# Two of the four sums of weight quarters made by accumulating DMAs in place of VectorE adds

## The chip, the cores and the metric

One core of a Trainium2 chip runs the whole program in one launch. The metric is the device time in microseconds; before the change the median of three runs is 2033.21 us (2032.05 to 2033.67). One execution was profiled.

## What is computed

Two decoder layers on 512 tokens of width 1024. Each has a feed-forward, a mixer and a second feed-forward; the mixer is gated linear attention in the first layer and latent attention in the second, with a cross-attention to 256 memory tokens beside it.

```python
for i in range(DEPTH):
    x = x + 0.5 * swiglu(rmsnorm(x, ffn1_norm[i]), ffn1_w_gate[i], ffn1_w_up[i], ffn1_w_down[i])
    h = rmsnorm(x, mix_norm[i])
    ...
    x = x + jnp.concatenate([o, o_mem], axis=-1) @ w_out[i]
    x = x + 0.5 * swiglu(rmsnorm(x, ffn2_norm[i]), ffn2_w_gate[i], ffn2_w_up[i], ffn2_w_down[i])

def swiglu(h, w_gate, w_up, w_down):
    return (jax.nn.silu(h @ w_gate) * (h @ w_up)) @ w_down
```

The change touches the weights of `w_gate` and `w_up` alone. Each of the four feed-forwards has 22 column blocks of 128 in each of them, taken two at a time: 44 groups in the program.

## The kernel before

All arithmetic is float32, made from pairs. A tile is split into a rounded high part (`fp32r`) and the rest, and a product is three matmuls: high by high, high by rest, rest by high (`mm3`). For a weight tile the high part `wh` is a cast on ScalarE and the rest `wl` a subtraction on VectorE; both read a raw tile of 128 by 1024 that a DMA from SP's queue brought from `wflat`, 512 KB.

The gate and up products of a group are made by a scheme with seven products in place of eight. The two weight blocks are cut into halves of the contracted width, which gives four quarters: a11 (gate, upper half), a21 (up, upper), a22 (up, lower), a12 (gate, lower). Seven left operands are made of them: a11, s1 = a21 + a22, s2 = s1 + a11, a12, s3 = a21 + a11, s4 = s2 + a12, and a22. VectorE makes the four sums, s3 in place on a21's raw tile, s1 and s2/s4 in two `sum` tiles. Each operand is split into `wh` and `wl` and used by 24 matmuls of 256 columns (`seven`, which also forms the sums of the activations in the same manner on VectorE and ScalarE: the tiles `t`). One group is thus 168 matmuls. Between groups stand steps of the down projection of the chunk of blocks before (`down`, with 512 columns and one plain weight unit per eight tiles), as `CHUNKS` and `SHARES` (lines 38 and 39) tell: none between the first two groups of a feed-forward, and one to three units between later ones.

The buffers are: four raw tiles, two sum tiles, four pairs of `wh` and `wl` (line 37). A raw tile's next load waits until its last reader is done; a pair is free once TensorE has made the product that reads it.

The order of each engine's queue is written by a planner in the kernel (`Flows`, lines 163 to 285): generators yield operations, the planner keeps a clock for each engine, prices every operation (`price`, line 140) and takes the one that can start first. The framework then moves instructions about by its own estimate when it writes the program. The queues are in order on the chip: an instruction that waits holds all that stands behind it on its engine. Since every operation is issued in `make` (line 136), all rows of the profile have that line, and are told apart by their tiles.

`load_unit` (line 348) issues one raw load per quarter or plain unit, and `split_weights` (line 357) makes sums and splits. `start` (line 1542) issues the first loads between the eight tiles of x.

Of the kernel before, what the change touches and what calls it, by code (L numbers as in the profile page):

```python
# [9 lines left out]
F32 = mybir.dt.float32  # L10
# [4 lines left out]
ALU = mybir.AluOpType  # L15
AX = mybir.AxisListType

P = 128
# [15 lines left out]
XH, XDH = 4, 128  # L34
UMAX = 1024
BLOCK = 256
NRAW, NSUM, NSPL, NTMP = 4, 2, 4, 31
CHUNKS = (4, 6, 4, 8)
SHARES = ((0, 0), (2, 2, 4), (4, 4), (2, 2, 2, 2))
HS = S // 2  # L40
# [60 lines left out]
def _n_free(a):  # L101
    return int(np.prod(a.shape[1:]))


def _in_psum(a):
    return a.space == bass.MemoryType.PSUM
# [13 lines left out]
class Engine:  # L120
# [19 lines left out]
    def price(self, method, kw, outs, ins):  # L140
        n = max([_n_free(outs[0])] + ([_n_free(ins[0])] if method == "tensor_reduce" else []))
        if self.name == "PE":
            if method == "transpose":
                return 110, 200
            n = _n_free(kw["rhs"])
            return (n / 2.4 + 13.3 if ins[0].dtype == F32R else 4 * n / 2.4 + 10), 200
        if self.name == "ACT":
            return 100 + 0.833 * n, 130
        if self.name == "POOL":
            return 100 + 2.2 * n, 200  # L150
        if method == "dma_start":
            return 60, 2000 + 4 * P * n / 360
        if method == "tensor_tensor_scan":
            return 70 + 2.1 * n, 130
        if method == "reciprocal":
            return 65 + 6 * n, 130
        single = method in ("tensor_scalar", "tensor_copy", "tensor_scalar_mul")
        if single and not any(_in_psum(a) for a in ins[:1] + outs[:1]):
            return 70 + 0.53 * n, 110
        return 70 + 1.042 * n, 110  # L160


class Flows:
# [7 lines left out]
    def spawn(self, gen, rank=1):  # L171
        self.count += 1
        self.flows.append([rank, self.count, gen, None, True])
# [4 lines left out]
    def done(self, *tiles):  # L178
        for t in tiles:
            if t.name in self.halves:  # L180
                h = self.halves[t.name]
                i = t.offset % UMAX // (UMAX // 2)
                assert h[2][i] is None
                h[2][i] = self.used(t.name, i * UMAX // 2, (i + 1) * UMAX // 2)
                if None not in h[2]:
                    del self.halves[t.name]
                    self.free_at["d"].append(max(h[2]))
            else:
                self.free_at[self.kind.pop(t.name)].append(self.used(t.name, 0, UMAX))
# [98 lines left out]
def _emit(tc, ctx, xT, memT, wflat, sizes, cst, out):  # L288
# [17 lines left out]
    V, A, G, T, Q = (Engine(e, n) for e, n in ((nc.vector, "DVE"), (nc.scalar, "ACT"), (nc.gpsimd, "POOL"),  # L306
                                               (nc.tensor, "PE"), (nc.sync, "SP")))
    spawn, done = fl.spawn, fl.done
# [3 lines left out]
    parts = [cs, None, None]  # L312

    def C(name, a=None, b=None):
        part, lo, hi = _C[name]
        if a is not None:
            lo, hi = lo + a, lo + b
        return parts[part][:, lo:hi]
# [21 lines left out]

    units = [[None, Flag()] for _ in sizes]
    outs = [[Flag(), None, n] for n, four in sizes for _ in range(7 if four == 1 else 1 if four == 0 else 0)]

    ahead = [0, 0]

    def load_unit():
        u, n = units[ahead[0]], sizes[ahead[0]][0]
        raw = yield Take("raw", F32, 0)  # L350
        o = ahead[1]
        yield Q.dma_start(out=raw[:, :n], in_=wflat[o : o + n * P].rearrange("(p n) -> p n", p=P))
        ahead[0] += 1
        ahead[1] += n * P
        u[0], u[1].set = raw, True

    def split_weights():
        def parts():
            h = yield Take("wh", F32R, 0)
            l = yield Take("wl", F32R, 0)  # L360
            return h, l

        def high(hl, src, n=UMAX):
            yield A.copy(out=hl[0][:, :n], in_=src[:, :n])

        def low(hl, src, n=UMAX):
            yield V.tensor_tensor(out=hl[1][:, :n], in0=src[:, :n], in1=hl[0][:, :n].bitcast(F32), op=ALU.subtract)
            o = outs[made[0]]
            made[0] += 1
            o[1], o[0].set = hl, True  # L370

        def add(out, a, b):
            yield V.tensor_tensor(out=out, in0=a, in1=b, op=ALU.add)

        todo = iter(zip(units, sizes))
        for u, (n, four) in todo:
            if four == 0:
                yield u[1]
                hl = yield from parts()
                yield from high(hl, u[0], n)  # L380
                yield from low(hl, u[0], n)
                done(u[0])
                continue
            u21, u22, u12 = (next(todo)[0] for _ in range(3))
            yield u[1]
            a11 = u[0]
            p = yield from parts()
            yield from high(p, a11)
            yield u21[1]
            yield u22[1]  # L390
            a21, a22 = u21[0], u22[0]
            s1 = yield Take("sum", F32, 0)
            yield from add(s1, a21, a22)
            yield from low(p, a11)
            p = yield from parts()
            yield from high(p, s1)
            s2 = yield Take("sum", F32, 0)
            yield from add(s2, s1, a11)
            yield from low(p, s1)
            done(s1)  # L400
            p = yield from parts()
            yield from high(p, s2)
            yield from add(a21, a21, a11)
            done(a11)
            yield from low(p, s2)
            yield u12[1]
            a12 = u12[0]
            p = yield from parts()
            yield from high(p, a12)
            yield from add(s2, s2, a12)  # L410
            yield from low(p, a12)
            done(a12)
            p = yield from parts()
            yield from high(p, a21)
            p2 = yield from parts()
            yield from high(p2, s2)
            yield from low(p, a21)
            done(a21)
            p = yield from parts()
            yield from high(p, a22)  # L420
            yield from low(p2, s2)
            done(s2)
            yield from low(p, a22)
            done(a22)

# [4 lines left out]
    class Blocks:  # L430
# [5 lines left out]
        def next(self):  # L436
            j = self.i % self.per
            if j == 0:
                self.end()
                u = outs[at[0]]  # L440
                assert u[2] == min(self.per, self.n - self.i) * self.w, at
                at[0] += 1
                yield u[0]
                self.cur = u[1]
            self.i += 1
            return tuple(t[:, j * self.w : (j + 1) * self.w] for t in self.cur)
# [67 lines left out]
    class Norm:  # L514
# [18 lines left out]
        def add(self, k):  # L533
            spawn(self.square(k), 1)
            yield from self.split(k)
# [134 lines left out]


    def seven(nrm, hid, f, start):

        made_, read = ({n: Flag() for n in ("p1", "p5", "u2", "p2", "u3", "p3", "p4")} for _ in range(2))
# [867 lines left out]
    def start():  # L1542
        yield V.memset(ones, 1.0)
        yield A.activation(out=warm, in_=ones[:, :1], func=AF.Silu)
        yield Q.dma_start(out=cs, in_=cst[:, : _PARTS[0]])
        spawn(split_weights(), lambda: 3 if made[0] - at[0] >= NAHEAD else -1)
        nrm = Norm("f1", 0)
        for k in range(KD):
            spawn(nrm.split(k), 0)
        for k in range(KD):  # L1550
            spawn(late_square(nrm, k))
        spawn(trunk(nrm), 2)
        yield from load_unit()
        for k in range(KD):
            yield Q.dma_start(out=x[k], in_=xT[:, k, :])
            xin[k].set = True
            if k in (3, 5, 7):
                yield from load_unit()
        yield V.tensor_scalar_mul(out=xqs, in0=C("xq"), scalar1=XDH ** -0.5)
        while ahead[0] < len(sizes):  # L1560
            yield from load_unit()

    def late_square(nrm, k):
        yield nrm.part[KD - 1]
        yield outs[NLATE][0]
        yield from nrm.square(k)

    def trunk(nrm):
        for l in range(2):
            nx = Norm("mx", l)  # L1570
            spawn(load_part(l + 1, nrm))
            yield from ffn(nrm, nx, False)
            nrm = Norm("f2", l)
            yield from (gla if l == 0 else mla)(l, nx, nrm)
            nx = Norm("f1", 1) if l == 0 else None
            yield from ffn(nrm, nx, l == 1)
            nrm = nx
# [160 lines left out]
```

## Time and profile before

| what | us |
|---|---|
| median of three runs | 2033.21 |
| the profiled execution's own time | 2034.4 |
| its span | 2032.6 |
| PE busy in the span | 2001.6 |
| DVE (VectorE) busy | 1595.5 |
| ACT (ScalarE) busy | 983.2 |
| POOL (GpSimd) busy | 49.1 |

PE is the row of the matmuls, PEld that of their weight loads, DVE is VectorE, ACT ScalarE, POOL GpSimd, SP the engine whose queue issues most DMAs. Busy shares are averages over stages with unlike limits, so the stages are looked at one by one. In a row of groups stand: line, engine, operation, tile written and tiles read, the shape, the count, then busy us and the mean ns of one, then the idle time of that engine just before them and what ended it. `sum<-raw` is s1, `raw<-raw` is s3, and `sum<-sum,raw` is s2 or s4.

### The profile page before, as it was taken

Reading aid. Unit: us, or ns where it says so; the run is one execution under the profiler, and the core shown is the slowest. Engines: PE = TensorE matmul, PEld = TensorE weight load, DVE = VectorE, ACT = ScalarE, POOL = GpSimd, SP = SyncE. Lnnn points to the kernel's source line nnn. Section 1 sums busy time; section 2 is a strip of 40 time slices with the busy share of each in tenths; the row PEclk is TensorE's granted clock in tenths of the full one; section 3 lists DMA queues with packets and bytes.
Section 4 is the critical chain, followed back from the end, with each engine's and each line's share of the span. In section 5 each row is a group of like instructions: output and inputs, shape, how many; then the busy total and the mean of one; then the engine's idle time right before and its main releaser. Section 6 shows DMA issues by size and latency. Waiting matters only on the chain.

```text
span 2032.6 us, 32247 instructions
## 1 busy us (share of the span) xinstructions
PE 2001.6 (98%) x12974; PEld 1804.4 (89%) x12974; DVE 1595.5 (78%) x2597; ACT 983.2 (48%) x1584; POOL 49.1 (2%) x121
## 2 busy tenths in 40 slices
PE   6999999999999999999999999999999999999999
PEld 6999998878888899999899999989877879998997
DVE  8996786647868899778799877865887769987782
ACT  6544454453442655344455444444576546543451
POOL 0000000000000000000000000010031100000000
PEclk8999999999999999999999999999999999999999
DMA  4233334322212233323323332333211212332231
GB/s 137 97 115 108 101 96 134 104 82 83 94 43 74 72 104 114 101 97 104 121 68 124 106 114 93 103 112 111 89 55 43 70 56 73 104 125 94 94 121 66
DMA packets 55589, 193.22 MB, mean 95 GB/s; under 512 B 6160, under 2 KB 7824, under 8 KB 55440
## 3 DMA queue, kind: packets, MB, share of 16 engines
q1 hardware_dynamic: 55152, 189.92, 28.4%
q8 instruction: 101, 1.65, 0.3%
q10 hardware_dynamic: 288, 1.26, 0.2%
q14 instruction: 48, 0.39, 0.1%
HBM read 189.05 MB, written 2.10 MB: 94 GB/s over the span
## 4 chain that ended last, share of the span: by engine, by line
PE 87%; DVE 9%; issue 1%; ACT 1%; DMA 0%; SPq 0%; POOL 0%; ACTq 0%; DVEq 0%; POOLq 0%
PE ps L136 87%; DVE t L136 4%; DVE wl L136 3%; DVE s L136 2%; DVE sum L136 1%; ACT t L136 1%; ACT wh L136 0%; DMA raw<-wflat 0%; DVE raw L136 0%; DVE x L136 0%; SPq L136 0%; POOL t L136 0%; DVE ps L136 0%; DVE rs L136 0%; ACTq L136 0%
## 5 line engine op out<-in xcount | busy, mean ns | idle before, releaser
L136 PE MATMUL ps<-t,wh 128*128 128x256 f32 (+1 forms) x6976 | 1537.8, 316 | 18.9 <-ACT t L136 12.5
L136 PEld LDWEIGHTS ps<-t,wh 128*128 128x128 f32 x6976 | 1158.0, 192 | 109.3 <-ACT t L136 13.8
L136 PE MATMUL ps<-t,wl 128*128 128x256 f32 (+1 forms) x3488 | 1100.8, 316 | 1.6 <-DVE wl L136 1.5
L136 PEld LDWEIGHTS ps<-t,wl 128*128 128x128 f32 x3488 | 668.2, 192 | 45.1 <-issue 3.5
L136 ACT CAST wh<-raw 128x1024 fp32r<-128x1024 f32 (+2 forms) x358 | 368.7, 1031 | 501.3 <-PE ps L136 379.1
L136 DVE TENSOR_TENSOR wl<-raw,wh 128x1024 fp32r<-128x1024 f32 (+2 forms) x358 | 428.5, 1199 | 112.1 <-ACT wh L136 111.4
L136 DVE TENSOR_TENSOR t<-t 128x512 f32<-128x512 f32 (+3 forms) x522 | 307.8, 611 | 13.6 <-ACT t L136 10.0
L136 ACT CAST wh<-sum 128x1024 fp32r<-128x1024 f32 x132 | 138.4, 1048 | 159.7 <-PE ps L136 108.9
L136 PE MATMUL ps<-wh,t 128*128 128x256 f32 (+3 forms) x928 | 215.4, 321 | 0.0
L136 DVE TENSOR_TENSOR wl<-sum,wh 128x1024 fp32r<-128x1024 f32 x132 | 160.9, 1219 | 55.4 <-ACT wh L136 55.4
L136 DVE SCALAR_TENSOR_TENSOR x<-ps,x 128x512 f32<-128x512 f32 x160 | 109.8, 686 | 104.0 <-PE ps L136 103.0
L136 ACT COPY t<-ps 128x512 f32<-128x512 f32 (+3 forms) x262 | 138.9, 534 | 58.9 <-PE ps L136 54.2
L136 DVE TENSOR_TENSOR t<-ps,t 128x512 f32<-128x512 f32 (+2 forms) x197 | 126.6, 645 | 48.4 <-PE ps L136 35.5
L136 PEld LDWEIGHTS ps<-wh,t 128*128 128x128 f32 x928 | 155.0, 190 | 9.4 <-issue 1.9
L136 PE MATMUL ps<-wl,t 128*128 128x256 f32 (+3 forms) x464 | 148.2, 319 | 0.0
L136 PE MATMUL ps<-t 128*128 128x128 f32 (+6 forms) x760 | 140.9, 329 | 0.9 <-ACT t L136 0.4
L136 ACT CAST t<-t 128x256 fp32r<-128x256 f32 (+1 forms) x208 | 99.2, 503 | 80.4 <-DVE t L136 80.2
L136 PEld LDWEIGHTS ps<-t 128*128 128x128 f32 (+1 forms) x760 | 99.1, 191 | 27.4 <-issue 12.6
L136 DVE SCALAR_TENSOR_TENSOR t<-t 128x512 f32<-128x512 f32 (+1 forms) x172 | 108.6, 634 | 12.8 <-ACT t L136 12.2
L136 ACT ACTIVATE t<-t 128x512 f32<-128x512 f32 x124 | 76.7, 630 | 66.8 <-DVE t L136 66.6
L136 DVE TENSOR_TENSOR sum<-sum,raw 128x1024 f32<-128x1024 f32 x88 | 107.0, 1216 | 0.1
L136 PEld LDWEIGHTS ps<-wl,t 128*128 128x128 f32 x464 | 88.2, 190 | 5.2 <-issue 1.2
(74 smaller groups left out, 769.7 us busy)
## 6 DMA issues: line engine op xcount, KB each, us to landing
raw<-wflat SPq DMA_DIRECT2D x342, 512.0 KB, 3.3
raw<-wflat SPq DMA_DIRECT2D x12, 192.0 KB, 2.3
x<-xT SPq DMA_DIRECT2D x8, 256.0 KB, 5.8
t<-memT SPq DMA_DIRECT2D x8, 256.0 KB, 3.4
out<-x SPq DMA_DIRECT2D x8, 256.0 KB, 2.0
raw<-wflat SPq DMA_DIRECT2D x4, 448.0 KB, 3.2
cm<-cst ACTq DMA_DIRECT2D x1, 640.0 KB, 5.5
cm<-cst ACTq DMA_DIRECT2D x1, 585.5 KB, 5.2
```

The source lines that it names most:

```text
L136: return Op(self.name, lambda: real(*args, **kw), cost, _places(ins), _places(outs), lat)
```

## The change

s1 and s3 are no longer made on VectorE. A quarter is loaded by SP's queue into a raw tile as before, and a second DMA, issued from POOL's queue with `accum_op=ALU.add`, adds another quarter from HBM to the same tile: a22 onto a21 for s1, a11 onto a21 for s3. a21 itself is not kept. POOL's DMA waits for the first one to land, and the readers of the tile wait for POOL's. A group has five raw tiles (a11, s1, a12, s3, a22), filled by seven transfers, where it had four filled by four. There are five raw tiles in place of four and one sum tile in place of two (s2, then s4). The planner prices a POOL DMA at 1000 ns on the engine, and the landing at 3000 ns and the bytes at 200 a ns after that.

```diff
-NRAW, NSUM, NSPL, NTMP = 4, 2, 4, 31
+NRAW, NSUM, NSPL, NTMP = 5, 1, 4, 31
...
+        if method == "dma_start" and self.name == "POOL":
+            return 1000, 3000 + 4 * P * n / 200
...
+    loads, at_ = [], 0
+    for n, four in sizes:
+        o = at_
+        at_ += n * P
+        if four == 0:
+            loads.append((n, (o,)))
+        elif four == 1:
+            q = [o + i * n * P for i in range(4)]
+            loads.extend((n, tuple(q[i] for i in t)) for t in ((0,), (1, 2), (3,), (1, 0), (2,)))
...
-        yield Q.dma_start(out=raw[:, :n], in_=wflat[o : o + n * P].rearrange("(p n) -> p n", p=P))
...
+        yield Q.dma_start(out=raw[:, :n], in_=src(places[0]))
+        for o in places[1:]:
+            yield G.dma_start(out=raw[:, :n], in_=src(o), accum_op=ALU.add)
...
-            yield u21[1]
-            yield u22[1]
-            a21, a22 = u21[0], u22[0]
-            s1 = yield Take("sum", F32, 0)
-            yield from add(s1, a21, a22)
             yield from low(p, a11)
+            yield u1[1]
+            s1 = u1[0]
             p = yield from parts()
             yield from high(p, s1)
             s2 = yield Take("sum", F32, 0)
             yield from add(s2, s1, a11)
+            done(a11)
             yield from low(p, s1)
             done(s1)
             p = yield from parts()
             yield from high(p, s2)
-            yield from add(a21, a21, a11)
-            done(a11)
-            yield from low(p, s2)
```

The change moves instructions on VectorE, at the start and in the feed-forwards, and gives POOL's queue the DMAs. The numbers behind the names tell the buffers apart. First VectorE in the first group. Before, from the first sum (`sum_139` is s1, `sum_147` s2, `raw_96` a11, `raw_123` a21, `raw_128` a22; `t` are tiles of the activations):

```order
L136 TENSOR_TENSOR sum_139<-raw_123,raw_128 128x1024
L136 TENSOR_TENSOR t_167<-t_104 128x256
L136 TENSOR_TENSOR sum_147<-sum_139,raw_96 128x1024
L136 TENSOR_TENSOR wl_144<-sum_139,wh_143 128x1024
L136 TENSOR_TENSOR t_106<-t_157,t_106 128x256
L136 TENSOR_TENSOR t_106<-t_167,t_106 128x256
L136 TENSOR_TENSOR t_167<-t_121 128x256 x2
L136 TENSOR_TENSOR raw_123<-raw_123,raw_96 128x1024
L136 TENSOR_TENSOR wl_153<-sum_147,wh_152 128x1024
```

Now (`raw_123` is s1 once both of its DMAs have landed, `sum_202` s2, `raw_131` a12):

```order
L136 TENSOR_TENSOR t_151<-t_129,t_104 128x256
L136 TENSOR_TENSOR t_108<-t_151,t_108 128x256
L136 SCALAR_TENSOR_TENSOR t_104<-t_168,t_129 128x256
L136 TENSOR_TENSOR sum_202<-raw_123,raw_96 128x1024
L136 TENSOR_TENSOR wl_146<-raw_123,wh_145 128x1024
L136 TENSOR_TENSOR t_189<-t_134,t_121 128x256
L136 TENSOR_TENSOR t_109<-t_168,t_109 128x256
L136 SCALAR_TENSOR_TENSOR t_151<-t_151,t_104 128x256
L136 SCALAR_TENSOR_TENSOR t_189<-t_189,t_121 128x256
L136 TENSOR_TENSOR t_168<-t_134,t_121 128x256
L136 TENSOR_TENSOR wl_209<-sum_202,wh_208 128x1024
```

The adds for s1 and s3 are gone, and more of the activations' `t` steps stand ahead of the first instruction that reads s1, which is the add for s2. From that add to the fourth sum's `wl` there were 34 of the `t` steps behind the first sum, and there are 28 behind the new first sum.

Second, VectorE late in the program, where one unit of the down projection stands between two groups. Now (`raw_18569` is a12 of one group, `raw_18582` its s3, `sum_18644` its s4, `raw_18625` its a22, `raw_18648` the down unit; `raw_18657` and `raw_18724` are a11 and s1 of the next group, `sum_18906` its s2):

```order
L136 TENSOR_TENSOR wl_18710<-raw_18569,wh_18709 128x1024
L136 TENSOR_TENSOR wl_18743<-raw_18582,wh_18742 128x1024
L136 TENSOR_TENSOR wl_18773<-sum_18644,wh_18772 128x1024
L136 TENSOR_TENSOR sum_18906<-raw_18724,raw_18657 128x1024
L136 TENSOR_TENSOR wl_18805<-raw_18625,wh_18804 128x1024
...
L136 TENSOR_TENSOR wl_18836<-raw_18648,wh_18835 128x1024
...
L136 TENSOR_TENSOR wl_18869<-raw_18657,wh_18868 128x1024
...
L136 TENSOR_TENSOR wl_18904<-raw_18724,wh_18903 128x1024
```

The add for the next group's s2 stands ahead of three other splits, that of this group's a22, of the down unit and of the next group's a11. `raw_18724` lies in the buffer that `raw_18569` had. In 17 of the 44 groups the add stands two `wl` rows behind the last reader of that buffer and three ahead of the `wl` of its own s1; in 8 it is two and two. Before, in a like place, with three down units between the groups (`raw_18470` is the new group's a11, `sum_18565` its s1, `sum_18607` its s2, `raw_18500` a21):

```order
L136 TENSOR_TENSOR wl_18556<-raw_18423,wh_18555 128x1024
...
L136 TENSOR_TENSOR sum_18565<-raw_18500,raw_18539 128x1024
...
L136 TENSOR_TENSOR wl_18563<-raw_18470,wh_18562 128x1024
...
L136 TENSOR_TENSOR sum_18607<-sum_18565,raw_18470 128x1024
L136 TENSOR_TENSOR wl_18605<-sum_18565,wh_18604 128x1024
L136 TENSOR_TENSOR raw_18500<-raw_18500,raw_18470 128x1024
...
L136 TENSOR_TENSOR wl_18632<-sum_18607,wh_18631 128x1024
```

There the first add stood directly ahead of the split of a11, the group's own.

Third, POOL's queue, which held after its first constants:

```order
L136 MEMSET t 128x512 x6
L136 ISA
L136 TENSOR_TENSOR t<-cm 128x128 x8
L136 TENSOR_TENSOR t<-t 128x128 x4
```

and now holds:

```order
L136 DMA raw<-wflat 128x1024 x22
L136 MEMSET t 128x512 x6
L136 DMA raw<-wflat 128x1024 x44
L136 ISA
L136 TENSOR_TENSOR t<-cm 128x128 x8
L136 TENSOR_TENSOR t<-t 128x128 x4
```

The last 22 of the 88 DMAs stand behind all of its other work. The rows of the mixers keep their order on the other engines but for a few.

More of the change, by code (lines that the diff above doesn't have):

```diff
@@ L338, in small, with src @@
         return sm.tile([P, 16], F32, tag="s", name="s")[:, :n]
-    units = [[None, Flag()] for _ in sizes]
+    loads, at_ = [], 0
[7 more added lines that the diff above has]
+            loads.extend((n, tuple(q[i] for i in t)) for t in ((0,), (1, 2), (3,), (1, 0), (2,)))
+    units = [[None, Flag()] for _ in loads]
     outs = [[Flag(), None, n] for n, four in sizes for _ in range(7 if four == 1 else 1 if four == 0 else 0)]
-    ahead = [0, 0]
+    ahead = [0]
     def load_unit():
-        u, n = units[ahead[0]], sizes[ahead[0]][0]
+        u, (n, places) = units[ahead[0]], loads[ahead[0]]
+        ahead[0] += 1
         raw = yield Take("raw", F32, 0)
-        o = ahead[1]
-        yield Q.dma_start(out=raw[:, :n], in_=wflat[o : o + n * P].rearrange("(p n) -> p n", p=P))
-        ahead[0] += 1
-        ahead[1] += n * P
+        def src(o):
+            return wflat[o : o + n * P].rearrange("(p n) -> p n", p=P)
+        yield Q.dma_start(out=raw[:, :n], in_=src(places[0]))
+        for o in places[1:]:
+            yield G.dma_start(out=raw[:, :n], in_=src(o), accum_op=ALU.add)
         u[0], u[1].set = raw, True
@@ L373, in add @@
             yield V.tensor_tensor(out=out, in0=a, in1=b, op=ALU.add)
-        todo = iter(zip(units, sizes))
-        for u, (n, four) in todo:
+        todo = iter(units)
+        for n, four in sizes:
+            if four < 0:
+                continue
+            u = next(todo)
             if four == 0:
@@ L383, in split_weights @@
                 continue
-            u21, u22, u12 = (next(todo)[0] for _ in range(3))
+            u1, u12, u3, u22 = (next(todo) for _ in range(4))
             yield u[1]
@@ L402, in split_weights @@
             yield from high(p, s2)
-            yield from add(a21, a21, a11)
-            done(a11)
-            yield from low(p, s2)
             yield u12[1]
             a12 = u12[0]
-            p = yield from parts()
[L409 to L414, printed above, removed]
+            p2 = yield from parts()
+            yield from high(p2, a12)
+            yield from low(p, s2)
+            yield from add(s2, s2, a12)
+            yield from low(p2, a12)
+            done(a12)
+            yield u3[1]
+            s3 = u3[0]
+            p = yield from parts()
+            yield from high(p, s3)
             p2 = yield from parts()
             yield from high(p2, s2)
-            yield from low(p, a21)
-            done(a21)
+            yield from low(p, s3)
+            done(s3)
+            yield from low(p2, s2)
+            done(s2)
+            yield u22[1]
+            a22 = u22[0]
             p = yield from parts()
             yield from high(p, a22)
-            yield from low(p2, s2)
-            done(s2)
             yield from low(p, a22)
@@ L1559, in start @@
         yield V.tensor_scalar_mul(out=xqs, in0=C("xq"), scalar1=XDH ** -0.5)
-        while ahead[0] < len(sizes):
+        while ahead[0] < len(loads):
             yield from load_unit()
```

## The prediction

> **What bounds the kernel now.** I read the page's first part, then a table of stretches, then the waits of the stretches where TensorE is not full.
>
> ```profile
> PE 2001.6 (98%) x12974; PEld 1804.4 (89%) x12974; DVE 1595.5 (78%) x2597; ACT 983.2 (48%) x1584; POOL 49.1 (2%) x121
> ```
>
> ```profile
> 13.00:36.00 23.00, 15.66 (x79) 13.46 (x78) 22.05 (x45) 17.54 (x38) 0.00 (x0) 0.78 0.27 91
> 36.00:110.00 74.00, 70.53 (x538) 67.53 (x537) 73.13 (x92) 39.70 (x54) 0.00 (x0) 0.98 0.30 98
> 110.00:340.00 230.00, 230.00 (x1599) 215.86 (x1599) 180.12 (x207) 103.64 (x130) 0.00 (x0) 1.00 0.34 111
> ...
> 640.00:690.00 50.00, 50.00 (x220) 40.97 (x219) 42.08 (x67) 21.27 (x36) 0.00 (x0) 1.00 0.25 85
> 700.00:775.00 75.00, 74.08 (x589) 72.24 (x589) 74.58 (x98) 43.01 (x61) 0.00 (x0) 1.00 0.30 99
> 1050.00:1100.00 50.00, 50.00 (x417) 49.85 (x417) 48.93 (x61) 28.05 (x37) 0.00 (x0) 1.00 0.36 118
> 1695.00:1765.00 70.00, 69.08 (x547) 67.24 (x547) 69.69 (x89) 39.13 (x51) 0.00 (x0) 1.00 0.29 96
> ```
>
> The columns are the stretch, its length, the busy time of PE, PEld, DVE, ACT and POOL with the number of instructions, the granted clock, the DMA share and GB/s. A busy PE need not be a full one, so I go by counts: 417 matmuls of 256 columns in 50 us are 0.120 us each, 220 of 512 columns are 0.227 us each, and the long feed-forward stretches (110 to 340) have no gap. There VectorE is busy for 180 of 230 us, and its adds cost nothing. VectorE has no room left in four places: 13 to 36 (22.05 of 23.00 us), 36 to 110 (73.13 of 74.00) and the starts of the two late feed-forwards (74.58 of 75.00, 69.69 of 70.00). Only there can fewer adds shorten the run. What TensorE lost in the second of them:
>
> ```profile
> L136 PE MATMUL ps<-t,wh 128*128 128x256 f32 x341 | 63.1, 285 | 1.6 <-ACT wh L136 1.2 <-ACT t L136 0.4
> L136 PE MATMUL ps<-t,wl 128*128 128x256 f32 x171 | 48.7, 285 | 1.6 <-DVE wl L136 1.5
> L136 PE MATMUL ps<-t,wh 128*128 128x512 f32 x16 | 6.3, 459 | 0.4 <-ACT t L136 0.4
> L136 PE MATMUL ps<-t,wl 128*128 128x512 f32 x8 | 3.8, 476 | 0.0
> L136 PE MATMUL ps<-t,ones 128*128 128x512 f32 x2 | 1.0, 592 | 0.0
> ```
>
> 512 short ones at 0.120 are 61.4 us, 24 long ones at 0.227 are 5.4, with 1.0 for the last row 67.8: 6.2 us of the 74 are lost. 3.5 of these are open gaps (74.00 - 70.53), and 1.5 the clock (2% of 74). The waits of the same stretch say whose gaps:
>
> ```profile
> ACT wh L136 <- DVE sum L136: 6.1, 4, 3.4
> ...
> PE ps L136 <- DVE wl L136: 1.5, 2, 0.9
> PE ps L136 <- ACT wh L136: 1.2, 1, 1.2
> PE ps L136 <- ACT t L136: 0.7, 2, 0.4
> ```
>
> ScalarE's cast waits for a sum, VectorE's `wl` is late because VectorE has a backlog: these gaps are the adds' doing.
>
> **What is removed.** Two rows of VectorE, by form, disappear: the first sum of each group and the third, made in place.
>
> ```profile
> L136 DVE TENSOR_TENSOR sum<-raw 128x1024 f32<-128x1024 f32 x44 | 53.6, 1218 | 3.0 <-DMA raw<-wflat 2.8
> ...
> L136 DVE TENSOR_TENSOR raw<-raw 128x1024 f32<-128x1024 f32 x44 | 53.5, 1217 | 0.0
> ```
>
> That is 107 us of busy time. On a queue without gaps one costs 1.14 us (12.82 to 13.96 below), so a group of seven products is relieved of 2.3 us.
>
> **Term one, 36 to 110.** Three groups run here, with three adds of each kind, and the first group's two lie ahead: by 100 us VectorE is 4 x 2.3 = 9.1 us earlier, more than every gap. The bound is 5.0 us (3.5 of gaps and 1.5 of clock, whose dip follows the gaps), and nothing at the other end; I take 4.5.
>
> **Term two, the first group.** VectorE works from the first sum to the end of the fourth without a gap.
>
> ```profile
> 12.82 1.23 DVE L136 TENSOR_TENSOR sum<-raw 128x1024 f32<-128x1024 f32 x1
> 13.96 0.42 DVE L136 TENSOR_TENSOR t<-t 128x256 f32<-128x256 f32 x1
> 14.29 1.22 DVE L136 TENSOR_TENSOR sum<-sum,raw 128x1024 f32<-128x1024 f32 x1
> ...
> 34.35 1.22 DVE L136 TENSOR_TENSOR wl<-sum,wh 128x1024 fp32r<-128x1024 f32 x1
> 35.49 0.42 DVE L136 TENSOR_TENSOR t<-t 128x256 fp32r<-128x256 f32 x1
> ```
>
> That is 22.7 us (12.82 to 35.49). In the new order two adds are gone (2.3 us) and six of the 34 small splits stand ahead of the wait instead of behind it (6 x 0.33 = 2.0), so 18.4 us remain, but they now begin when the sum that the DMAs make has landed, since `sum_202<-raw_123,raw_96` stands in VectorE's queue and everything behind it waits. It breaks even if that sum lands at 17.1 us, and each us later or earlier is a us of the start. When does it land?
>
> ```profile
> GB/s 0 0 0 0 65 296 156 287 287 384 359 287 302 241 205 302 394 399 415 389 399 369 307 323 353 369 389 410 394 394 394 420 435 435 384 154 51 0 0 0
> ```
>
> ```profile
> 5.02 7.78 DMA raw<-wflat
> ```
>
> ```profile
> raw<-wflat SPq DMA_DIRECT2D x342, 512.0 KB, 3.3
> ```
>
> ```profile
> DMA to landing us min/median/max: 3.1/3.3/4.9
> ```
>
> The first row is the traffic of the first 16 us in slices of 0.4 us, the second the third weight load (issued at 5.02, landed at 12.80), the third the usual load, the fourth the loads of 1764 to 2000 us. The second load stands 1024 KB ahead of the third in SP's queue, 2.7 us at some 390 GB/s, so it lands at about 10. The trace shows no accumulating transfer. It is at least a plain load, 3.3 us. It must also fetch the tile that it adds to, another 512 KB (1.3 us), and be issued by POOL behind a wait (SP's issues take some 0.4): 5.0 us, my value alone. In the first 14 us the transfer shares the engines with the x tiles and the other loads, 1.5 us more: 6.5, so 16.5 us, and the start gains 0.6. From above I bound it by twice the slowest of these loads, 9.8 us: between 3.8 gained (13.3) and 2.7 lost (19.8).
>
> **Term three, the late feed-forwards.** Each of the two other full stretches shows TensorE idle for 0.92 us, of which the same row in both is due to a sum:
>
> ```profile
> PE ps L136 <- ACT wh L136: 0.4, 1, 0.4
> ```
>
> At most 0.8, at least nothing; I take 0.4.
>
> **What is added, and what covers it.** 88 accumulating transfers and 44 more plain loads, with 69 MB more from HBM; the engines stand at 0.36 of their time at most in the stretches above, and I cost the traffic at nothing. POOL's queue in this part of the program holds only these DMAs and six memsets; its mixer work stands behind loads that are long done. The cover of the latency is the lookahead: five raw tiles, four split pairs. With one down-projection unit between two groups, `sum_18906` stands between the split of the fourth sum and that of a22 in VectorE's queue. A product takes 24 x 0.120 = 2.9 us. Its split needs a cast and a subtraction.
>
> ```profile
> L136 ACT CAST wh<-raw 128x1024 fp32r<-128x1024 f32 x342 | 358.9, 1050 | 486.5 <-PE ps L136 376.6 <-issue 103.5 <-DMA raw<-wflat 2.7
> ...
> L136 DVE TENSOR_TENSOR wl<-raw,wh 128x1024 fp32r<-128x1024 f32 x342 | 417.7, 1223 | 111.4 <-ACT wh L136 111.1
> ```
>
> Count from the end of the down unit, when a pair comes free for a12: a12 is split 2.4 us later (1.05 and 1.22 with the hand-overs), its raw tile takes the next group's first load (3.3), and the accumulation takes L more: the sum is there at 5.7 + L. a22 is wanted by TensorE after a11, s1, s2, a12, s3 and s4, at 6 x 2.9 = 17.3, and behind the add come 1.14 and 1.22 us of VectorE. So L may be 9.2 us before TensorE waits. The split of a22 could begin at 9.7 (after s2 and a cast: 3 x 2.9 and 1.05), so from about 4 us on VectorE stands idle at the add, with gates and splits behind it; its spare 50 of 230 us pay for that. 17 of the 44 groups stand so; the others have more distance. Without cover, at the upper bound of 9.8, 17 x 0.6 = 10 us are lost.
>
> By the Trainium skill, SBUF — State Buffer, Who interferes with whom, a DMA from the GpSimd queue is starved of its descriptors while VectorE holds the shared port pair in a 2-port operation. By the same section `tensor_tensor` takes only the pair's read side, and descriptor generation needs the write side (inferred there). By that the lock is no matter here; no run so far shows it. The 2-port candidates in the full stretches are a few rows such as
>
> ```profile
> L136 DVE TENSOR_SCALAR t<-t 128x512 int32<-128x512 int32 x2 | 0.8, 419 | 0.0
> ```
>
> which would add under half a us to one transfer.
>
> **The sum.** 4.5 + 0.6 + 0.4 = 5.5 us. The profiled execution took 2034.4 us (span 2032.6), 1.2 above the median of the runs, 2033.21; so 2028.9 for an execution like it, 2027.7 as a median. The best ends give 5.0 + 3.8 + 0.8 = 9.6, 2023.6.
>
> **Rivals.**
>
> *The start gives the gain back.* If POOL's first transfer takes 9 us or more, the first sum lands near 19.5, 2.4 us are lost there, and the rest gains 4.9: 2.5 us, 2030.7. For it: the engines are full until about 14 us, and x6, x7 and a12 are delayed by the new traffic too. Against it: the second load lands early. Here belongs a first term that shrinks because the sums of these groups are late as well.
>
> *The add blocks VectorE's queue.* Where L exceeds 9.2 us, every one of the 17 groups pays the excess; at 11 us 17 x 1.8 = 31 us, less the 5.5: 2058.7. It decides from 9.5 us on, where 17 x 0.3 cancel the gain. For it: the sum of the next group has been put ahead of a split that TensorE wants soon, and nothing shows the price of an accumulation. Against it: it would take nearly three times a plain load.
>
> *VectorE shuts POOL out.* If POOL cannot issue while VectorE runs two-input operations, the first group and the three after it, where VectorE has no gap, get their sums only once VectorE stands at the add: 4 x 5.0 us, less 4 x 2.3, 11 us: 2044. For it: 73.13 of 74.00 us. Against it: POOL's few instructions of the mixers ran beside VectorE, and nothing in the trace shows the lock. The skill's section named above speaks against it for `tensor_tensor`.
>
> **How the numbers follow.** Forecast 0.47, the start gives back 0.28, the add blocks 0.19, POOL shut out 0.06. About 0.2%, 4.1 us, is what a measurement of this kernel can tell from no change. The forecast is faster, the first rival the same, the two others slower: 0.47, 0.28, 0.25. The range begins at the best ends, 2023.6, and reaches into the slower cases up to the bound of 9.8 us and a little further (2033.2 + 10 - 5.5 = 2038, and 2044 for the third rival): 2042. The likeliest case alone runs from 2023.6 to 2029.1.
>
> **What would show it.** On VectorE 88 rows fewer, and the first `sum<-raw` at about 16.5 us; in 36 to 110 TensorE busy for nearly all of the time, with the clock at 1.00; an accumulation landing 5 to 6.5 us after its issue. In 110 to 340 VectorE's adds wait for a DMA by a us or two, with TensorE still at 230 of 230. The prediction is wrong if TensorE waits for `wl` or `wh` in the long stretches, or if the first sum lands after 19 us.

## The result, and the profile after

The changed kernel is slower: 2065.8 us median of four runs (2062.2 to 2071.7) against 2032.7 of the kernel before, a ratio of 1.0165 with a 95% interval of 1.0138 to 1.0193. The forecast was 2027.7. The profiled execution took 2062.2 us, that of before 2034.4: the two traces show 28 of the 33 us.

VectorE does less, as planned, and TensorE is not the better for it. The page's first part, and of its groups the add for s2 (now the first reader of s1), the silu on ScalarE and POOL's DMAs (count, busy us, mean ns, then the idle time ahead of them and what ended it):

```profile
PE 2006.1 (97%) x12974; PEld 1806.3 (88%) x12974; DVE 1500.8 (73%) x2509; ACT 976.0 (47%) x1584; POOL 124.1 (6%) x209
...
L136 ACT ACTIVATE t<-t 128x512 f32<-128x512 f32 x124 | 76.6, 630 | 165.3 <-DVE t L136 165.1
L136 POOL DMA_DIRECT2D raw<-wflat x88 | 76.1, 865 | 1300.2 <-DVE t L136 535.4
...
L136 DVE TENSOR_TENSOR sum<-raw 128x1024 f32<-128x1024 f32 x44 | 53.9, 1225 | 127.3 <-DMA raw<-wflat 127.1
```

VectorE has 88 rows fewer (2509 for 2597) and 95 us less to do, but stands idle for 127.1 us at the adds for s2, before a DMA. The stretches show where TensorE lost by it (columns as before):

```profile
36.00:110.00 74.00, 72.45 (x573) 70.51 (x573) 70.92 (x94) 42.07 (x58) 5.18 (x6) 1.00 0.62 166
110.00:340.00 230.00, 222.25 (x1537) 208.57 (x1537) 159.07 (x186) 98.35 (x125) 11.21 (x13) 0.99 0.55 151
...
775.00:1000.00 225.00, 218.92 (x1559) 206.52 (x1558) 156.12 (x180) 99.25 (x125) 12.08 (x14) 1.00 0.53 150
```

In 36 to 110 TensorE now makes 573 matmuls where it made 538, at full clock: the relief came. In 110 to 340, full before (230.00, x1599), it has 7.75 us of gaps, and in 775 to 1000 another 6.08. Before the change both stretches were full (230.00 and 225.00 us busy). VectorE is idle for 71 of the 230 us in the first. The waits of the whole run, first before, then after:

```profile
ACT t L136 <- DVE t L136: 157.9, 156, 4.2
...
PE ps L136 <- ACT t L136: 14.7, 11, 7.8
```

```profile
ACT t L136 <- DVE t L136: 246.9, 142, 7.0
...
DVE sum L136 <- DMA raw<-wflat: 127.1, 34, 5.5
...
PE ps L136 <- ACT t L136: 36.2, 27, 8.0
```

In the long stretches TensorE does not wait for weights: from 110 to 340 all that its matmuls wait for is ScalarE's `t` (7.8 us, five times). ScalarE waits for VectorE's `t`, and VectorE for the transfer. The accounts close: I summed, over all matmuls, the time from one start to the next above the median of its kind. That sum rose by 27.4 us, and the span by 27.8 (2060.4 for 2032.6). By stretch it is 3.0 lost up to 50 us, 4.4 gained from 50 to 100, and 28.8 lost after 100 (59.5 for 30.7). Some 25 of these 28.8 lie at 19 gaps of 0.3 to 3.4 us ended by ScalarE's `t` in the feed-forwards: 15 of the gaps in the 17 groups where the add stands two `wl` rows behind the buffer's last reader and three ahead of its own, none in the 8 with two and two, four in others. Another 3.6 went by in two stretches in which the granted clock was 0.5 (140.2 to 147.0 and 1300.8 to 1304.2 us), during or just behind a gap.

One of these gaps, 138 to 142 us, in a group with two down units ahead of the next, engine by engine (start, duration, engine, instruction; in brackets the idle time ahead of it and what ended it):

```profile
132.81 0.86 POOL L136 DMA_DIRECT2D raw<-wflat  x1 [18.72 <-DMA raw<-wflat]
...
132.59 0.69 DVE L136 TENSOR_TENSOR t<-ps,t 128x512 f32<-128x512 f32 x1 [0.70 <-PE ps L136]
138.67 1.22 DVE L136 TENSOR_TENSOR sum<-raw 128x1024 f32<-128x1024 f32 x1 [5.39 <-DMA raw<-wflat]
139.81 0.69 DVE L136 TENSOR_TENSOR t<-t 128x512 f32<-128x512 f32 x1
...
140.53 0.63 ACT L136 ACTIVATE t<-t 128x512 f32<-128x512 f32 x1 [7.02 <-DVE t L136]
141.07 0.57 ACT L136 COPY t<-ps 128x512 f32<-128x512 f32 x1
...
141.69 0.80 PE L136 MATMUL ps<-t,wh 128*128 128x256 f32 x2 [3.38 <-ACT t L136]
```

The gate of a finished half begins on VectorE at 132.59. Its next step, the scaling, could follow at 133.2, but the add for the next group's s2 stands between them in the queue and waits 5.39 us. The scaling comes at 139.81 and ScalarE's silu at 140.53. Behind the silu in ScalarE's queue stands the copy of u3 (what the fifth product made) out of PSUM, long possible, at 141.07. The seventh product (p4) goes into the PSUM bank that this copy empties, so TensorE starts it at 141.69. The first matmuls after that start 0.21 us apart in place of 0.12, at the granted clock of 0.5. VectorE, ScalarE and TensorE stood in line for one transfer, each with an instruction that had nothing to do with it.

### The profile page after: what moved, and what is told of

It reads as the page before. It is cut to its first block, busy times and chain, and to the rows that moved or that the text cites. A ratio compares the mean times of both kernels' runs of the same rounds, so it can differ in the third digit from the quotient of the medians.

```text
span 2060.4 us, 32560 instructions
## 1 busy us (share of the span) xinstructions
PE 2006.1 (97%) x12974; PEld 1806.3 (88%) x12974; DVE 1500.8 (73%) x2509; ACT 976.0 (47%) x1584; POOL 124.1 (6%) x209
## 3 DMA queue, kind: packets, MB, share of 16 engines
q1 hardware_dynamic: 61488, 212.99, 30.7%
## 5 line engine op out<-in xcount | busy, mean ns | idle before, releaser
L136 ACT CAST wh<-raw 128x1024 fp32r<-128x1024 f32 (+2 forms) x402 | 413.9, 1032 | 543.3 <-PE ps L136 409.9
L136 DVE TENSOR_TENSOR wl<-raw,wh 128x1024 fp32r<-128x1024 f32 (+2 forms) x402 | 483.4, 1204 | 114.9 <-ACT wh L136 110.2
L136 POOL DMA_DIRECT2D raw<-wflat x88 | 76.1, 865 | 1300.2 <-DVE t L136 535.4
L136 ACT COPY t<-ps 128x512 f32<-128x512 f32 (+3 forms) x262 | 138.7, 533 | 33.2 <-PE ps L136 28.8
L136 DVE TENSOR_TENSOR wl<-sum,wh 128x1024 fp32r<-128x1024 f32 x88 | 107.6, 1223 | 56.1 <-ACT wh L136 55.7
L136 DVE TENSOR_TENSOR sum<-raw 128x1024 f32<-128x1024 f32 x44 | 53.9, 1225 | 127.3 <-DMA raw<-wflat 127.1
L136 ACT CAST wh<-sum 128x1024 fp32r<-128x1024 f32 x88 | 92.1, 1047 | 91.4 <-PE ps L136 71.2
```

Source lines behind the costliest of these rows:

```text
L136: return Op(self.name, lambda: real(*args, **kw), cost, _places(ins), _places(outs), lat)
```

## Experiments

The theory (A): the add for s2 waits at the head of VectorE's in-order queue for the accumulated s1, and what stands behind it is late. Its rivals: the added traffic slows what runs beside it (B); POOL's issues and VectorE hinder each other (C). "Lost after 100" is the sum above, beyond 100 us; it was 30.7 before the change, all but some 2 us of it outside the long feed-forward stretches, and 59.5 after it.

**The add moved back.** An edge of order only: the framework had put the add ahead of splits and gates that the planner had written before it; here it may not pass the `wl` of its own group's a11.

```diff
             yield from low(p, a11)                      # its instruction is kept in `cell`
...
-            yield from add(s2, s1, a11)
+            yield from add(s2, s1, a11, behind=cell)    # order only: behind that `wl` on VectorE
```

> The changed kernel with one edge of order more: the add for a group's s2 is put on VectorE's queue behind the `wl` of the same group's a11, so that the splits of the group before, of the down unit and of a11, and the gates among them, stand ahead of it. The transfers are the same. Theory A (the add waits at the head of VectorE's queue for the accumulated s1, and gates and splits are late behind it): TensorE's time lost after 100 us falls from some 28 us above the kernel before to under 6, VectorE's wait of sums for DMA from 127 us to under 30, time 2030 to 2040 (the start keeps its 4.6 us of loss, 50 to 100 us its 4.5 of gain). Theory B (the added transfers themselves slow what runs beside them): 2058 to 2068, as the changed kernel. Theory C (POOL's issues and VectorE hinder each other): also 2058 to 2068, since both work as much as before.

2030.2 us, ratio 0.9988 (0.9979 to 0.9997). From its waits and its stretches:

```profile
PE ps L136 <- ACT t L136: 14.9, 9, 8.1
...
DVE sum L136 <- DMA raw<-wflat: 6.5, 2, 5.4
```

```profile
36.00:110.00 74.00, 72.45 (x566) 70.66 (x566) 70.34 (x92) 41.34 (x56) 5.18 (x6) 0.98 0.64 167
110.00:340.00 230.00, 230.00 (x1591) 215.48 (x1590) 164.10 (x191) 104.40 (x131) 11.21 (x13) 1.00 0.55 155
700.00:775.00 75.00, 74.97 (x603) 73.81 (x602) 69.58 (x90) 41.72 (x54) 5.18 (x6) 1.00 0.64 176
1695.00:1765.00 70.00, 70.00 (x564) 69.04 (x563) 64.21 (x81) 39.90 (x51) 6.00 (x7) 1.00 0.66 177
```

With the same 88 transfers and the same share of the DMA engines (0.55), TensorE is full again from 110 to 340, and 27.2 us are lost after 100. B and C fall: nothing of the transfers had to go. The change's 33 us were a matter of where one instruction of each group stood.

**By the gate or by the weights?** The add stays in place and waits as before; on ScalarE the silu is put behind the copy of u3.

```diff
+            if name == "p2":
+                yield read["u3"]          # and an edge of order: behind the copy of u3 on ScalarE
             yield A.activation(out=g, in_=g, func=AF.Silu)
```

> The changed kernel with one edge on ScalarE alone: the silu of the fourth product's half is put behind the copy of the fifth product (u3) out of PSUM. The add for s2 stands where it stood, ahead of three `wl` in 17 groups, and waits as long. It tells the two ways apart in which the waiting add can reach TensorE. By the gate (the scaling behind the add is late, so the silu is, so the copy behind the silu on ScalarE is, so the seventh product, which reuses that copy's PSUM bank, is): most of the 27 us lost after 100 us go though VectorE's sums still wait some 100 us for DMA; 2030 to 2042. By the weights (the `wl` of a22 behind the add is late): nothing changes for TensorE, 2055 to 2068.

2039.6 us (2035.6 to 2045.0), 1.0039 (1.0024 to 1.0054). Waits:

```profile
DVE sum L136 <- DMA raw<-wflat: 121.8, 33, 6.8
...
PE ps L136 <- ACT t L136: 14.7, 9, 7.9
...
PE ps L136 <- DVE wl L136: 2.8, 5, 0.7
```

VectorE still waits 121.8 us, but 26 of the 33 us are gone: the gate, the silu and the copy behind it were the way to TensorE. The new edge also moved the add back by one `wl` row in the 8 groups with two and two; none of the gaps lay in these. For any `wl` TensorE waits 2.8 us in all. The profiled execution (2035.6) was the shortest of five; where the rest of the 7 us goes in the longer ones is not shown.

**How long the landing may take.** Three kernels with the add where the change has it (17 to 19 groups stand two `wl` behind and three ahead), and other transfers. Each has one of the three new lines; the kernels with 64 and 768 columns leave the rest of the sums unmade, the plain one makes no sums at all.

```diff
-            yield G.dma_start(out=raw[:, :n], in_=src(o), accum_op=ALU.add)
+            yield G.dma_start(out=raw[:, :64], in_=src(o)[:, :64], accum_op=ALU.add)      # 64 columns
+            yield G.dma_start(out=raw[:, :768], in_=src(o)[:, :768], accum_op=ALU.add)    # 768 columns
+            yield G.dma_start(out=raw[:, :n], in_=src(o))                                 # plain
```

> The changed kernel, its accumulating transfers cut from 1024 columns to 64, so that the sums s1 and s3 are left unmade in the other 960 columns: the same issues and waits at a sixteenth of the bytes. Theory A: what counts is how long the sum takes to land; if an accumulation of 32 KB lands some 3 us after its issue in place of 6.1, half of the waits go, and with them more than half of the 33 us, since only what exceeds the cover is lost: 2032 to 2045. Theory B (bytes): 2030 to 2036. Theory C (POOL's issue): 2058 to 2068, since the 88 issues stay.

> The changed kernel, each accumulating transfer made a plain one from the same queue (the second quarter overwrites the first, so s1 and s3 are no sums): the order on all engines is the same row for row. It parts what adding costs in the transfer from what the second transfer in POOL's queue costs. If adding is what makes it long: landing 3.5 to 4.5 us after the issue in place of 6.1, and by theory A 2036 to 2050. If the two transfers in a row and POOL's queue make it long: landing at 5.5 to 6.5, time 2055 to 2068. Theory B (bytes): the read of the tile that is added to goes, a third of the added traffic on the SBUF side; 2050 to 2060.

> The changed kernel, its accumulating transfers cut to 768 of 1024 columns (s1 and s3 unmade in the other 256); in 17 groups the add stands ahead of three `wl`, as in the changed kernel. Landing after the issue was 3.1 us for 64 columns (no loss after 100 us) and 6.1 for 1024 (27 us lost). If the landing grows in proportion, it is about 5.2 us here. Theory A with a break-even near 4.5 us (where plain transfers landed, with some 3 us lost): 25 or more groups are over it by up to 0.7 us at the median and by more in the tail, 5 to 15 us lost, 2035 to 2047. If the loss goes in proportion to the bytes: 2050 to 2056.

The landings after POOL's issue, from the views of the raw tile on POOL: 64 columns, then plain, then 768 columns, then the changed kernel.

```profile
DMA to landing us min/median/max: 2.4/3.1/6.5
```

```profile
DMA to landing us min/median/max: 3.5/4.5/8.0
```

```profile
DMA to landing us min/median/max: 4.5/5.6/8.1
```

```profile
DMA to landing us min/median/max: 5.2/6.1/8.9
```

| transfer from POOL | median landing | VectorE's wait at the adds | lost after 100 | time | ratio |
|---|---|---|---|---|---|
| 64 columns, accumulating | 3.1 | 42.6 | 26.6 | 2028.9 | 0.9983 (0.9974 to 0.9992) |
| 1024 columns, plain | 4.5 | 72.1 | 29.1 | 2031.4 | 0.9997 (0.9988 to 1.0007) |
| 768 columns, accumulating | 5.6 | 118.8 | 51.8 | 2055.0 | 1.0111 (1.0097 to 1.0124) |
| 1024 columns, accumulating | 6.1 | 127.1 | 59.5 | 2065.8 | 1.0165 (1.0138 to 1.0193) |

The loss is a threshold, not a slope: up to a median of 4.5 us VectorE's waits (72 us of them) cost TensorE 2 us or so; the next 1.1 us cost 23. With 768 columns some 19 us are lost at 17 gaps of the feed-forwards, 14 of them in the 17 groups named above and none in the 8. My expectations by A were too high for the first two, where I had the loss begin earlier, and too low for the third, whose landing was longer (5.6 for 5.2) and whose gaps cost 1.1 us each on average. The third time, 2055.0, lies in the range that I gave for a loss in proportion to the bytes. But the loss does not go by bytes: the plain transfer brings as many from HBM as the full accumulation and loses next to nothing, and the kernel with the add moved back moves all the bytes of the change.

**One part alone.** s1 by accumulation, s3 on VectorE in place:

```diff
-            loads.extend((n, tuple(q[i] for i in t)) for t in ((0,), (1, 2), (3,), (1, 0), (2,)))
+            loads.extend((n, tuple(q[i] for i in t)) for t in ((0,), (1, 2), (1,), (3,), (2,)))
...
+            yield u3[1]
+            s3 = u3[0]
+            yield from add(s3, s3, a11)
```

> The changed kernel with s1 alone made by an accumulating transfer; s3 is made by VectorE in place on a21's tile, as in the kernel before (six transfers in place of seven, five raw tiles, 44 accumulations). Theory A: the waits come from s1, which VectorE's add for s2 waits for; VectorE gets 54 us of adds back, so it is no faster than the changed kernel: 2055 to 2072. Theories B and C (in proportion to transfers): half of the loss, 2045 to 2052.

2064.8 us, 1.0159 (1.0140 to 1.0178): half the accumulations, all of the loss, 58.2 us lost after 100. Now s3 alone, on the kernel before, onto the tile of a21 that is there anyway:

```diff
             yield from add(s1, a21, a22)
+            yield G.dma_start(out=a21, in_=u[2], accum_op=ALU.add)    # u[2]: a11 in wflat
...
-            yield from add(a21, a21, a11)
```

> The kernel before with s3 alone made by a DMA: s1 on VectorE as before, then an accumulating transfer of a11 onto a21's own tile in place of VectorE's third add (four loads and one accumulation a group, four raw and two sum tiles as before). No add of VectorE waits for an accumulation then; only ScalarE's cast and the `wl` of s3 do, three products (8.7 us) after s1, against some 7 us from the add of s1 to the landing. Theory A (harm comes from an in-order queue that waits): no harm beyond 3 us where the landing is late, and about half of the relief of 36 to 110 us: 2030 to 2034. If accumulating transfers do harm wherever they are: half of the changed kernel's loss, 2045 to 2052.

2026.3 us, 0.9972 (0.9962 to 0.9981): faster than both kernels. Its waits and stretches:

```profile
PE ps L136 <- ACT t L136: 12.8, 7, 8.1
...
DVE sum L136 <- DMA raw<-wflat: 2.4, 3, 1.2
```

```profile
36.00:110.00 74.00, 72.37 (x572) 70.28 (x572) 72.58 (x93) 39.22 (x54) 2.60 (x3) 1.00 0.48 137
110.00:340.00 230.00, 230.00 (x1576) 214.89 (x1576) 171.15 (x198) 103.75 (x129) 6.58 (x8) 1.00 0.42 123
...
1695.00:1765.00 70.00, 70.00 (x560) 68.83 (x559) 67.93 (x83) 39.56 (x51) 2.58 (x3) 1.00 0.50 137
```

So the harm is s1's, which an add of VectorE waits for early; s3 is wanted three products after its tile is ready to be added to. One add per group less is relief enough for 36 to 110 (572 matmuls, 573 with two adds less). I had expected 2030 at best, because I had not counted the first group, which ends earlier by it (below).

**The start.** Three kernels with the add moved back, and another first group: both of its sums on VectorE (four loads); its second load two x tiles earlier; s1 on VectorE and s3 accumulated onto a21.

```diff
+            loads.extend(...)             # first group: ((0,), (), (1,), (2,), (3,)), () a tile without a load
...
+            if one:
+                yield from add(s1, u3[0], u22[0])
```

```diff
-            if k in (3, 5, 7):
+            if k in (1, 5, 7):
```

> The reordered kernel (add for s2 behind the `wl` of a11) with the first group's s1 and s3 made on VectorE as in the kernel before (four loads), the other 43 groups by accumulation. If the late landing of the first sum (19.4 us, against an add at 12.8 before) is what the start loses, matmul 168 starts at some 44.7 us as before, in place of 46.7, and the time is 2027.5 to 2029.5. If the start's loss has another source (the loads' order, the casts), 2029.5 to 2031.

> The reordered kernel with the first two quarters of the first sum loaded two x tiles earlier (after the second x tile in place of the fourth). If the first sum's landing sets the start, it lands some 1.3 us earlier (512 KB at 390 GB/s), near 18 us, and the time is 2028.5 to 2030. If the x tiles set it, they come 1.3 us later and the time is 2030 to 2032.

> The reordered kernel with the first group's s1 on VectorE and its s3 by an accumulating transfer onto a21's tile, the other 43 groups by accumulation. It joins the start of the kernel in which only s3 is made by a DMA (matmul 168 at 42.5 us, against 43.5 with both sums of the first group on VectorE) to the reordered feed-forwards. If the gains add up: 2025 to 2027. If the start with accumulating transfers from the second group on brings its own loss: 2027 to 2029.

| first group | first sum ready for the splits | matmul 168 starts | granted clock, 13 to 50 us | lost to the clock before matmul 168 | time | ratio |
|---|---|---|---|---|---|---|
| before the change | 14.0 | 44.7 | 0.86 | 3.9 | 2032.1 to 2032.7 | 1 |
| add moved back, else as the change | 19.4 | 46.7 | 0.82 | 3.6 | 2030.2 | 0.9988 (0.9979 to 0.9997) |
| second load earlier | 17.9 | 45.2 | 0.91 | 1.9 | 2030.7 | 0.9991 (0.9982 to 1.0000) |
| s1 on VectorE, s3 accumulated | 14.1 | 44.5 | 0.82 | 6.0 | 2028.8 | 0.9979 (0.9970 to 0.9988) |
| both sums on VectorE | 14.9 | 43.5 | 0.91 | 3.3 | 2026.5 | 0.9971 (0.9959 to 0.9982) |
| s3 alone, all groups | 14.0 | 42.5 | 0.95 | 1.5 | 2026.3 | 0.9972 (0.9962 to 0.9981) |

Matmul 168 is about the end of the first group. The clock was granted at 0.5 or 1.0 in these traces, and the fifth column is an estimate of what the half clock cost: over the matmuls that start in its stretches, the time to the next start above the median of the kind, without idle time.

With both sums of the first group on VectorE that group ends 3.2 us earlier, at nearly the same loss to the clock, and the time falls by 3.7: the accumulation in the first group was all that kept the reordered kernel from a gain like that of s3 alone. Both were a little more than I had expected (44.7, and 2027.5 at best). With its loads moved ahead the first sum landed 1.5 us earlier; that gave 1.5 us at matmul 168 in the profile, and nothing in the median. The profile is that of the shortest of its eleven runs, and the clock can account for its 1.5 us (1.9 lost for 3.6). The median lies in the range that I gave for the case that the x tiles set the start, which no run tests.

Joining the two better starts did not add up in the median, and the clock is the likely reason. In the joined kernel's profile matmul 168 comes 2 us after that of s3 alone, but 6.0 us are lost to the clock there and 1.5 in the other; without that it would be ahead. The runs agree: at a mean granted clock of 0.997 the joined kernel took 2026.1 to 2028.8 us (four runs) and the kernel with s3 alone 2027.6 to 2028.8 (three runs). Seven of the ten runs of s3 alone had 0.998 or more, and none of the eleven of the joined kernel. Why the clock comes up later in some starts is open.

## Why the prediction was wrong

**What is removed** held: 88 rows of VectorE are gone, with 95 us of its busy time for the 107 reckoned.

**Term one, 36 to 110** (4.5 us, at most 5.0) held. From the start of matmul 168 to that of 800 the kernel before takes 87.6 us, the changed one 84.2, the one with the add moved back 83.4: 3.4 to 4.2 gained, a little under the 4.5. At 130 us the changed kernel was 2.1 us ahead (matmul 800 at 130.2 for 132.3).

**Term two, the first group** (0.6 gained, range to 2.7 lost) had the sign wrong: matmul 168 starts 1.3 us later, 46.0 for 44.7. The second load was there at about 10.4 as worked out (POOL's DMA is issued at 10.48), but the accumulation took 8.7 us more, not 6.5. On VectorE and TensorE:

```profile
19.20 1.23 DVE L136 TENSOR_TENSOR sum<-raw 128x1024 f32<-128x1024 f32 x1 [5.15 <-DMA raw<-wflat]
```

```profile
20.30 0.79 PE L136 MATMUL ps<-t,wh 128*128 128x256 f32 x2 [6.57 <-ACT wh L136]
```

It lands at 19.2, past the 19 that the prediction named as a sign of being wrong. The break-even of 17.1 can't be read off directly: with 64 columns the sum was there at 16.6, and matmul 168 started no earlier (46.0). But 5.0 us were lost there to the granted clock of 0.5, against 3.9 before the change and 3.3 after it (estimates, as in the table above). Without them it is 41.0 for 40.8 before and 42.7 after, which fits a break-even near 17.

**Term three, the late feed-forwards** (0.4 of 0.8) is real where nothing else goes wrong: with the add moved back, 700 to 775 shows 74.97 busy and 1695 to 1765 shows 70.00, where 74.08 and 69.08 stood. In the changed kernel it does not appear: from 700 to 775 TensorE still waits 0.6 us for a `wl` and 0.4 for VectorE's `t`, while VectorE works without a wait for a transfer. Why is open.

**The added traffic at nothing** held: the same traffic runs beside a full TensorE once the add is moved.

**The cover** is the step that failed. Its count of the time to the sum was 2.2 us short: in the gap shown above SP's load for the tile was issued at 128.1, POOL's accumulation at 132.8, and the sum was there at 138.6, 10.5 us in place of 3.3 + 5.0. That alone would have broken nothing by its own limit, L of 9.2 for a22's weights, and for the 13 of the 17 groups that have one down unit in between, as the limit supposes, no run speaks against it: where the gate's way is cut, TensorE waits 2.8 us for `wl` in the whole run. The other four have two down units, and there it is lower: at 141.9 in that run TensorE waits 0.67 us for a `wl` behind the add, with an L of 6.55. That VectorE would stand idle at the add was seen too, "from about 4 us" (at 3.1 us it already did, for 42.6 us). The wrong clause is the next: "its spare 50 of 230 us pay for that". Spare time is a mean over 230 us and pays for work, not for a deadline. The gate's scaling behind the add has one, by way of a silu and a copy, some 3 us after it could start: in the gap shown, the add would have had to begin at 135.1 (scaling to matmul takes 1.9 us, and TensorE was ready at 138.2), and began at 138.7. The prediction named the gates behind the add and priced only the `wl`.

**The size of L** (5.0, bounds 3.3 to 9.8) was too small by a fifth (6.1 at the median). A plain transfer from POOL's queue takes 4.5 where the forecast had 3.3 from SP's, and adding takes 1.6 more where it had 1.3. The runs put the point from which the waits cost time between medians of 4.5 and 5.6, so the 5.0 of the forecast stood on the edge itself, with 17 groups to fall.

**The rivals.** The second, that the add blocks VectorE's queue, is what happened; it named the place and set the point from which it decides at 9.5 us, about twice too high, for the reason above. The first, that the start gives the gain back, took place as well, at 1.3 us in place of 2.4. The third, that VectorE shuts POOL out, did not show. With the add moved back VectorE is busy for 70.34 of the 74 us from 36 to 110, and the six accumulations issued there land at a median of 6.0 us, against 6.1 for the 13 from 110 to 340:

```profile
raw<-wflat POOLq DMA_DIRECT2D x6, 512.0 KB, 6.0
```

```profile
raw<-wflat POOLq DMA_DIRECT2D x13, 512.0 KB, 6.1
```

That agrees with what the Trainium skill, SBUF — State Buffer, Who interferes with whom, says of `tensor_tensor`: that it did not stall such a transfer.

## What to carry to other kernels

When an operand is moved from an engine to a transfer, look up where its first reader stands in that engine's queue, list everything behind it, and give each of these its own deadline, through every in-order queue that it feeds, up to the engine that must not stop. Idle time on the blocked engine, however much, is not cover. If a scheduler places the reader by its own idea of the landing, tie it down with an edge of order, or choose the operand whose reader comes late: here s3 gains 6 us by a DMA, and s1 loses 33.

## What the runs showed of the hardware

An accumulating transfer of 512 KB from POOL's queue takes 5.2 us from issue to landing at the shortest, where a plain one from the same queue takes 3.5 and one of 32 KB that accumulates 2.4; so adding costs some 1.7 us at 512 KB. The accumulating transfer takes longer with more bytes (2.4, 4.5 and 5.2 us at 32, 384 and 512 KB). POOL is busy with its issue for 0.86 us if it accumulates and for 0.53 if it is plain. By the Trainium skill, DMA: Bandwidth & Descriptors, Anatomy of one DMA — SWDGE (gpsimd) path, a transfer from this queue takes 2.0 us and its bytes at 436 KB a us, by estimate 3.2 for 512 KB: the plain transfer at its shortest (3.5) comes near, and the accumulating one takes 2 us more than the estimate.
